# Gate and up pairs that move both parts of x side by side, and a pool product issued ahead of the scans

## The chip, the cores and the metric

The kernel runs on one core of one Trainium2 chip. The time is device time in microseconds (us) from one launch to its end; the median over runs is what is compared. In the profile TensorE is PE (its weight loads are PEld), VectorE is DVE, ScalarE is ACT, GpSimd is POOL, and SyncE is SP, which issues most of the transfers.

## The reference, cut to what matters

Two layers. Each is a feed-forward block, a mixer, and a second feed-forward block, each between two norms:

```python
for l in range(2):                                      # x: 256 tokens x 1024
    f = _swiglu(_rmsnorm(h, ff1_norm_pre[l]), wg, wu, wd)     # 1024 -> 2816 -> 1024
    h = h + 0.5 * _rmsnorm(f, ff1_norm_post[l])
    m = _hybrid_mixer(_rmsnorm(h, mix_norm_pre[l]), ...)
    h = h + _rmsnorm(m, mix_norm_post[l])
    f = _swiglu(_rmsnorm(h, ff2_norm_pre[l]), ...)
    h = h + 0.5 * _rmsnorm(f, ff2_norm_post[l])

def _swiglu(h, wg, wu, wd):
    return (silu(h @ wg) * (h @ wu)) @ wd

def _hybrid_mixer(h, w_in, ..., w_out):
    z, xbc, dt, u, q, k, v = split(h @ w_in)
    y_ssd  = _ssd_mixer(z, xbc, dt, ...)     # two chunks of 128 tokens, a state carried between them
    y_pool = _pool_mixer(u, pool_w, pool_scale)   # windowed means of u, minus u, times pool_w
    y_attn = _moba_attention(q, k, v)        # 256 tokens: one causal block
    return concatenate([y_ssd, y_pool, y_attn]) @ w_out
```

All inputs are float32. The kernel gets the precision from two-part products: every weight and every activation is held as a high part (`hi`, rounded to the format that TensorE takes) and a low part (`lo`, the rest), and a product is `hi.hi + hi.lo + lo.hi`.

## The kernel before

**Weights.** A weight unit is a tile `raw` of 128 x 2048 that SP loads. ACT copies it to `hi` (L104) and DVE subtracts to `lo` (L105). Four `raw` tiles and five pairs `hi`, `lo` exist at a time; `W.pump()` splits further units whenever a pair is free, so these splits run ahead of TensorE up to five units. Every split sits in the queues of ACT and DVE between the evacuations of the products.

**Feed-forward.** The 2816 hidden columns are eleven groups of 256. Groups 0 and 1 go token tile by token tile (`ffn_first`, L340). Groups in `QUADS = (2, 5, 8)` are taken two at a time as seven products of combined weights (`ffn_quad`, L469, with DVE sums at L103). Groups in `PAIRS = (4, 7, 10)` go through `ffn_pair`: gate unit `p["g", i]`, the transposes of the hidden values that were made before (`turn`, L446), up unit `p["u", i]`, and then the gate: SiLU of the gate bank on ACT (L417), its product with the up bank on DVE (L419), and a split of the result into `hT`. There are four feed-forwards and so twelve pairs. In a pair the products are made by `mm_feat` (L319): for each half of 128 columns (`j`) 24 matmuls of 256 columns, weight stationary, x turned (`xT`) moving, all into one accumulator of 256 columns: 8 for `hi` with the high part of x, 8 for `hi` with its low part, 8 for `lo` with the high part. So each `hi` tile is loaded twice. Down products (`mm_rows`, L358, into the banks called `acc`) follow.

**Mixer.** Late in the mixer stands a group of work that is ordered with `issue_after`: `scan(0)` and `scan(1)` (L926) are TensorE products of the two token chunks, `carry()` (L917, evacuated by DVE at L896 and L919) brings the state of chunk 0 into chunk 1, `gated` (L934 to L938) multiplies by silu(z) and normalizes, giving `yn0` and `yn1`, and the pool product (L967) gives `y_pool` after two scalings on ACT (L869) and a split (L219, L220). The output product then adds up, for token tile 0 and then for tile 1, the attention rows (`wa`), the pool rows (`wp`) and two SSD units (`ws0`, `ws1`), each 12 matmuls of 512 columns at L358. `gated_turn` transposes `yn0` and `yn1` for the SSD units (L944). When tile 0 is complete, `post(0)` normalizes it and adds it to `h`, the next block's pre-norm makes `xn0` (L227 squares and sums, L229 adds eps, POOL takes the power at L232, L251 updates `h`, L260 scales), and `pre_turn` transposes `xn0` (L270). That transpose is pinned in the middle of tile 1's last unit:

```python
mm_rows(acc[1], p["ws1"], 1, y_ssd[1], False, True, joint)    # joint: pre_turn(0, xn0)
```

**What sets the order.** The code is written in program order, with hints (`issue_after`); a list scheduler at build time then sets the order of each engine's queue, within the dependencies, and each engine runs its queue strictly in that order. Banks called `wk` and `acc` are two sets of four accumulators of 512 columns, and a new one waits until the last reader of the old one is done.

Of the kernel before, what the change touches and what calls it, by code (L numbers as in the profile page):

```python
# [11 lines left out]
F32R = mybir.dt.float32r  # L12
BF16 = mybir.dt.bfloat16
AF = mybir.ActivationFunctionType
ALU = mybir.AluOpType
AX = mybir.AxisListType

P = 128
D = 1024
S = 256  # L20
NT = S // P
DEPTH = 2
KD = D // P
# [6 lines left out]
UNIT = 2048  # L30
# [11 lines left out]
V_CW, V_CB, V_PS, V_PW = 0, 32, 40, 42  # L42
# [98 lines left out]
def hybrid_trunk_kernel(ctx: ExitStack, tc: tile.TileContext, a, out: bass.AP):  # L141
    nc = tc.nc
    consts = ctx.enter_context(tc.tile_pool(name="consts", bufs=1))
# [8 lines left out]
    def buf(dtype=F32, n=512, tag="t"):  # L152
        return tmp.tile([P, n], dtype, tag=tag, name=f"{tag}{next(ids)}", bufs={"t": 20, "n": 8}[tag])
# [4 lines left out]
    def bank(tag="wk"):  # L158
        return psum.tile([P, 512], F32, tag=tag, name=f"{tag}{next(ids)}")
# [4 lines left out]
    W = Weights(nc, rawp, splitp)  # L164
# [42 lines left out]
        nc.scalar.activation(neg_b, cst[:, C_NEG : C_NEG + P], AF.Copy)  # L207

    gains = consts.tile([P, 2, D], F32, name="gains")
    xT = [consts.tile([P, KD, S], F32R, name=f"xT{i}") for i in range(2)]  # L210

    def load_gain(which, l, n):
        row = a["gains"][l, n : n + 1, :]
# [99 lines left out]
    def mm_feat(ps, u, c, x=xT, ncols=256):  # L313

        hi, lo = (w[:, : KD * ncols].rearrange("p (k n) -> p k n", k=KD) for w in W.get(u))
        s = slice(c, c + P)
        for i, (w, y) in enumerate(((hi, x[0]), (hi, x[1]), (lo, x[0]))):
            for k in range(KD):
                nc.tensor.matmul(ps, w[:, k, s], y[:, k, :], start=i == 0 and k == 0, stop=i == 2 and k == KD - 1)  # L319

    def mm_tok(ps, u, t, ncols=256):

# [91 lines left out]
    def gate(pg, pu, s=None):  # L414
        if s is None:
            s = buf()
            nc.scalar.activation(s, pg, AF.Silu)  # L417
        hf = buf()
        nc.vector.tensor_tensor(hf, pu, s, op=ALU.mult)  # L419
        return hf  # L420
# [26 lines left out]
            split_into(hT[i], (slice(None), slice(None)), ps)  # L447

    def ffn_pair(i, p, turn):
        pg, pu = bank(), bank()  # L450
        for ps, k in ((pg, "g"), (pu, "u")):
            for j in range(2):
                mm_feat(ps[:, j * 256 : (j + 1) * 256], p[k, i], j * P)
            W.done(p[k, i])
            if k == "g":
                turn()
        hf = gate(pg, pu)
        hT = (buf(F32R), buf(F32R))
        split_into(hT, (slice(None), slice(None)), hf)
        W.pump()  # L460
        return hT
# [152 lines left out]
    def mixer(l, p, turned, next_left, before_next):  # L614
# [93 lines left out]
        turn = []  # L708
        for w in range(2):
            ps = bank("acc")  # L710
# [210 lines left out]
        def scan(t):  # L921
            ps = bank()
            for hd in range(HEADS):
                s = slice(hd * 64, (hd + 1) * 64)
                n = hd % 4
                scan.last = nc.tensor.matmul(ps[:, s], decay[t, hd // 4][:, n * P : (n + 1) * P], xdt[t][:, s],  # L926
                                             start=True, stop=True)
            return ps
# [27 lines left out]
        with tc.issue_after(turn_x.last.ins):  # L956
            sz1 = zed(1)
        with tc.issue_after(zed.last.ins):
            y0 = scan(0)
            yn0 = gated(0, y0, sz0)  # L960
            carry()
            y1 = scan(1)

            pp = bank("acc")
            pw = vec[:, V_PW : V_PW + 256].rearrange("p (j n) -> p j n", j=2)
            for j in range(2):
                m = nc.tensor.matmul(pp[:, j * 256 : (j + 1) * 256], pw[:, j, :], d[:, j, :], start=True, stop=True)  # L967
            y_pool = rows_out(pp, vec[:, V_PS : V_PS + 2])
            yn1 = gated(1, y1, sz1)
        acc = [banks2(), banks2()]  # L970
        with tc.issue_after(m.ins):
            mm_rows(acc[0], p["wa"], 0, y_attn, True, False)
        m = mm_rows(acc[0], p["wp"], 0, y_pool, False, False)
        with tc.issue_after(m.ins):
# [189 lines left out]
```

## Time and profile before

| | |
|---|---|
| time, median of 3 runs | 931.28 us (930.87 to 931.46) |
| the profiled execution, its own time | 931.69 us |
| its span, first to last instruction | 930.0 us |
| mean granted TensorE clock | 0.997 |
| PE busy | 917.9 us, 5058 matmuls |
| DVE busy | 785.5 us, 1019 instructions |
| ACT busy | 584.2 us, 931 instructions |
| POOL busy | 30.1 us, 49 instructions |
| memory | 190.54 MB in packets, mean 205 GB/s |

The span is 1.69 us shorter than the same execution's time, and that execution lies 0.41 us above the median. A matmul's duration in the profile overlaps the next one, so what a matmul costs in a row of them is read from start to start.

### The profile page before, as it was taken

Reading aid. Unit: us, or ns where it says so; the run is one execution under the profiler, and the core shown is the slowest. Engines: PE = TensorE matmul, PEld = TensorE weight load, DVE = VectorE, ACT = ScalarE, POOL = GpSimd, SP = SyncE. Lnnn points to the kernel's source line nnn. Section 1 sums busy time; section 2 is a strip of 40 time slices with the busy share of each in tenths; the row PEclk is TensorE's granted clock in tenths of the full one; section 3 lists DMA queues with packets and bytes.
Section 4 is the critical chain, followed back from the end, with each engine's and each line's share of the span. In section 5 each row is a group of like instructions: output and inputs, shape, how many; then the busy total and the mean of one; then the engine's idle time right before and its main releaser. Section 6 shows DMA issues by size and latency. Waiting matters only on the chain.

```text
span 930.0 us, 13066 instructions
## 1 busy us (share of the span) xinstructions
PE 917.9 (99%) x5058; PEld 794.0 (85%) x5058; DVE 785.5 (84%) x1019; ACT 584.2 (63%) x931; POOL 30.1 (3%) x49
## 2 busy tenths in 40 slices
PE   7999999999999999999999999999999999999997
PEld 5889898989988888888888988898998888989895
DVE  6999999589868998988599989876989699989872
ACT  7665747478738665646566756556794567656641
POOL 0000000000001000000000000000000110000000
PEclk9999999999999999999999999999999999999999
DMA  8576958465434486848455968583834246868521
GB/s 325 153 274 201 386 157 314 179 215 194 181 109 173 103 304 190 318 135 305 148 181 156 342 171 289 165 315 110 297 104 172 72 145 185 319 203 270 188 101 45
DMA packets 28002, 190.54 MB, mean 205 GB/s; under 512 B 3106, under 2 KB 3362, under 8 KB 5924
## 3 DMA queue, kind: packets, MB, share of 16 engines
q1 hardware_dynamic: 26068, 176.87, 52.1%
q0 software_dynamic: 1728, 12.58, 7.5%
q8 instruction: 39, 0.64, 0.3%
q10 hardware_dynamic: 144, 0.26, 0.1%
q14 instruction: 23, 0.19, 0.1%
HBM read 188.65 MB, written 1.05 MB: 204 GB/s over the span
## 4 chain that ended last, share of the span: by engine, by line
PE 95%; issue 1%; DVE 1%; DMA 1%; ACT 1%; POOL 0%; DVEq 0%; POOLq 0%; SPq 0%; ACTq 0%
PE acc L358 29%; PE wk L469 25%; PE wk L319 21%; PE wk L340 14%; PE wk L446 2%; PE wk L327 1%; PE wk L270 1%; DMA raw<-in_ff_f 1%; DVE lo L105 0%; PE acc L677 0%; PE acc L747 0%; ACT hi L104 0%; ACT n L227 0%; PE acc L879 0%; PE wk L905 0%
## 5 line engine op out<-in xcount | busy, mean ns | idle before, releaser
L104 ACT ACTIVATE hi<-raw 128x1024 fp32r<-128x1024 f32 (+2 forms) x452 | 401.1, 938 | 176.9 <-DVE raw L103 44.6
L105 DVE TENSOR_TENSOR lo<-raw,hi 128x1024 fp32r<-128x1024 f32 (+2 forms) x452 | 467.1, 1079 | 51.5 <-ACT hi L104 50.2
L358 PE MATMUL acc<-hi,t 128*128 128x512 f32 x832 | 216.2, 391 | 0.5 <-DVE t L896 0.5
L358 PEld LDWEIGHTS acc<-hi,t 128*128 128x128 f32 x832 | 154.8, 188 | 32.7 <-DVE t L896 1.4
L319 PE MATMUL wk<-xT,hi 128*128 128x256 f32 x1088 | 143.4, 284 | 0.0
L319 PEld LDWEIGHTS wk<-xT,hi 128*128 128x128 f32 x1088 | 136.7, 191 | 1.7
L358 PE MATMUL acc<-lo,t 128*128 128x512 f32 x416 | 114.1, 390 | 0.0
L469 PE MATMUL wk<-hi,n 128*128 128x512 f32 x384 | 102.9, 390 | 0.0
L340 PE MATMUL wk<-hi,xT 128*128 128x512 f32 x384 | 99.0, 395 | 2.6 <-ACT hi L104 2.6
L358 PEld LDWEIGHTS acc<-lo,t 128*128 128x128 f32 x416 | 78.0, 188 | 16.2
L103 DVE TENSOR_TENSOR raw<-raw,raw 128x1024 f32<-128x1024 f32 x72 | 86.2, 1219 | 1.9 <-DMA raw<-in_ff_q 1.9
L340 PEld LDWEIGHTS wk<-hi,xT 128*128 128x128 f32 x384 | 71.6, 189 | 17.6 <-ACT hi L104 3.4
L469 PEld LDWEIGHTS wk<-hi,n 128*128 128x128 f32 x384 | 71.8, 188 | 14.7
L469 PE MATMUL wk<-hi,xT 128*128 128x512 f32 x288 | 77.8, 392 | 0.0
L319 PE MATMUL wk<-xT,lo 128*128 128x256 f32 x544 | 76.8, 283 | 0.0
L319 PEld LDWEIGHTS wk<-xT,lo 128*128 128x128 f32 x544 | 70.3, 192 | 0.0
L469 PEld LDWEIGHTS wk<-hi,xT 128*128 128x128 f32 x288 | 53.5, 188 | 12.6 <-DVE t L502 1.8
L340 PE MATMUL wk<-lo,xT 128*128 128x512 f32 x192 | 52.3, 395 | 0.0
L469 PE MATMUL wk<-lo,n 128*128 128x512 f32 x192 | 51.3, 389 | 0.0
L244 DVE TENSOR_TENSOR n<-acc,gains 128x512 f32<-128x512 f32 x24 | 16.1, 689 | 33.6 <-ACT n L227 33.6
L340 PEld LDWEIGHTS wk<-lo,xT 128*128 128x128 f32 x192 | 36.6, 191 | 7.8
L469 PEld LDWEIGHTS wk<-lo,n 128*128 128x128 f32 x192 | 36.0, 188 | 7.5
(175 smaller groups left out, 731.2 us busy)
## 6 DMA issues: line engine op xcount, KB each, us to landing
raw<-in_ff_q SPq DMA_DIRECT2D x48, 1024.0 KB, 5.0
raw<-in_ff_d SPq DMA_DIRECT2D x44, 1024.0 KB, 5.0
raw<-in_ff_f SPq DMA_DIRECT2D x16, 1024.0 KB, 6.2
raw<-in_ff_q POOLq DMA_DIRECT2D x12, 1024.0 KB, 8.0
raw<-in_ff_g SPq DMA_DIRECT2D x12, 1024.0 KB, 4.8
raw<-in_ff_u SPq DMA_DIRECT2D x12, 1024.0 KB, 4.9
raw<-in_w_in SPq DMA_DIRECT2D x10, 1024.0 KB, 4.8
raw<-in_w_kvz SPq DMA_DIRECT2D x8, 1024.0 KB, 5.0
```

What stands on the lines that cost most here:

```text
L103: nc.vector.tensor_tensor(raw[:, s], self.raw[x][:, s], self.raw[y][:, s], op=op)
L104: self.act = nc.scalar.activation(hi[:, s], raw[:, s], AF.Copy)
L105: nc.vector.tensor_tensor(lo[:, s], raw[:, s], hi[:, s].bitcast(F32), op=ALU.subtract)
L244: nc.vector.tensor_tensor(fg[i], f[i], gains[:, 1, i * 512 : (i + 1) * 512], op=ALU.mult)
L270: pre_turn.last = nc.tensor.transpose(ps[:, k * P : (k + 1) * P], xn[i][:, k * P : (k + 1) * P], ident)
L319: nc.tensor.matmul(ps, w[:, k, s], y[:, k, :], start=i == 0 and k == 0, stop=i == 2 and k == KD - 1)
L327: nc.tensor.matmul(ps, x[:, k, s], w[:, k, :], start=i == 0 and k == 0, stop=i == 2 and k == KD - 1)
L340: m = nc.tensor.matmul(ps, y[:, k, :], w[:, k, :], start=h == 0 and n == 0, stop=h == 1 and n == len(parts) - 1)
L358: m = nc.tensor.matmul(acc[b], x[:, j, s], w[:, j, b * 512 : (b + 1) * 512], start=first and j == 0 and i == 0, stop=last and j == 1 and i ...
L446: nc.tensor.transpose(ps[:, j * S + t * P : j * S + (t + 1) * P], hf[t][:, c], ident)
L469: nc.tensor.matmul(ps, x[:, k, :], w[:, k, :], start=first and n == 0, stop=n == len(parts) - 1, skip_group_check=not first)
```

## The change

In `ffn_pair`, `mm_feat` is replaced by a new `mm_side`. The two parts of xT now lie in one tile, and `hi` moves both at once: 8 matmuls of 512 columns into one bank, the left half `hi.hi`, the right half `hi.lo`; 8 matmuls of 256 columns add `lo.hi` into the right half. ACT copies the right half out (L334) and DVE adds the left half to it (L335). This is done per 128 columns, so a unit takes two banks instead of one. SiLU and the product with the up values are now done on the summed copies.

```diff
-    xT = [consts.tile([P, KD, S], F32R, name=f"xT{i}") for i in range(2)]
+    both = consts.tile([P, 2, KD, S], F32R, name="xT")
+    xT = [both[:, i] for i in range(2)]
...
+    def mm_side(u, out):
+        hi, lo = (w[:, :UNIT].rearrange("p (k n) -> p k n", k=KD) for w in W.get(u))
+        for j in range(2):
+            s = slice(j * P, (j + 1) * P)
+            ps = bank()
+            for k in range(KD):
+                nc.tensor.matmul(ps, hi[:, k, s], both[:, :, k, :], start=k == 0, stop=k == KD - 1)
+            for k in range(KD):
+                nc.tensor.matmul(ps[:, S:], lo[:, k, s], xT[0][:, k, :], start=False, stop=k == KD - 1,
+                                 skip_group_check=True)
+            o = out[:, j * S : (j + 1) * S]
+            nc.scalar.activation(o, ps[:, S:], AF.Copy)
+            nc.vector.tensor_tensor(o, ps[:, :S], o, op=ALU.add)
+        W.done(u)
+        return out
...
     def ffn_pair(i, p, turn):
-        pg, pu = bank(), bank()
-        for ps, k in ((pg, "g"), (pu, "u")):
-            for j in range(2):
-                mm_feat(ps[:, j * 256 : (j + 1) * 256], p[k, i], j * P)
-            W.done(p[k, i])
-            if k == "g":
-                turn()
-        hf = gate(pg, pu)
+        s = mm_side(p["g", i], buf())
+        nc.scalar.activation(s, s, AF.Silu)
+        turn()
+        hf = mm_side(p["u", i], buf())
+        nc.vector.tensor_tensor(hf, hf, s, op=ALU.mult)
...
         with tc.issue_after(zed.last.ins):
+            pp = bank("acc")
+            pw = vec[:, V_PW : V_PW + 256].rearrange("p (j n) -> p j n", j=2)
+            for j in range(2):
+                pooled = nc.tensor.matmul(pp[:, j * 256 : (j + 1) * 256], pw[:, j, :], d[:, j, :], start=True, stop=True)
+            y_pool = rows_out(pp, vec[:, V_PS : V_PS + 2])
+        with tc.issue_after(pooled.ins):
             y0 = scan(0)
             yn0 = gated(0, y0, sz0)
             carry()
             y1 = scan(1)
-            pp = bank("acc")
-            ...
-            y_pool = rows_out(pp, vec[:, V_PS : V_PS + 2])
             yn1 = gated(1, y1, sz1)
         acc = [banks2(), banks2()]
-        with tc.issue_after(m.ins):
+        with tc.issue_after(scan.last.ins):
             mm_rows(acc[0], p["wa"], 0, y_attn, True, False)
```

The queues that come out of it differ as follows; line numbers are each version's own (L319 and L340 keep the meaning given above before; after the change L329 and L331 are the two loops of `mm_side`, L358 is `mm_half`, L376 is `mm_rows`, L271 the transposes of `xn`, L464 those of `hf`). Numbers behind a name count buffers.

PE, the first pair (group 4) of the second feed-forward, before: gate unit, the eight transposes of the hidden values, start of the up unit.

```order
L469 MATMUL wk_3098<-hi_3199,n_3119 128x512 x4
L319 MATMUL wk_3329<-xT_108,hi_3222 128x256 x8
L319 MATMUL wk_3329<-xT_109,hi_3222 128x256 x8
L319 MATMUL wk_3329<-xT_108,lo_3223 128x256 x8
L319 MATMUL wk_3329<-xT_108,hi_3222 128x256 x8
L319 MATMUL wk_3329<-xT_109,hi_3222 128x256 x8
L319 MATMUL wk_3329<-xT_108,lo_3223 128x256 x8
L446 MATMUL wk_3379<-ident,t_3242 128x128
```

The same place now.

```order
L484 MATMUL wk_3031<-hi_3132,n_3052 128x512 x4
L329 MATMUL wk_3263<-xT,hi_3155 128x512 x8
L331 MATMUL wk_3263<-xT,lo_3156 128x256 x8
L329 MATMUL wk_3282<-xT,hi_3155 128x512 x8
L331 MATMUL wk_3282<-xT,lo_3156 128x256 x8
L464 MATMUL wk_3302<-ident,t_3175 128x128
```

A unit's 48 matmuls of 256 columns have become 16 of 512 and 16 of 256, in two banks; nothing else moved there.

PE, the scan group of the first mixer, before (`t_2510` is the pooled difference d, `vec` holds pool_w).

```order
L926 MATMUL wk_2596<-t_2534,n_2272 128x64 x4
L926 MATMUL wk_2596<-t_2534,n_2277 128x64 x4
L917 MATMUL acc_2616<-t_2536,t_2306 128x256
L917 MATMUL acc_2616<-t_2536,t_2312 128x256
L926 MATMUL wk_2622<-t_2545,n_2282 128x64 x4
L926 MATMUL wk_2622<-t_2545,n_2287 128x64 x4
L967 MATMUL acc_2631<-t_2510,vec_860 128x256 x2
L358 MATMUL acc_2652<-hi_2295,t_2525 128x512
```

The same place now.

```order
L358 MATMUL wk_2482<-hi_2136,xT 128x512 x4
L977 MATMUL acc_2529<-t_2443,vec_837 128x256 x2
L941 MATMUL wk_2539<-t_2467,n_2205 128x64 x4
L941 MATMUL wk_2539<-t_2467,n_2210 128x64 x4
L932 MATMUL acc_2559<-t_2469,t_2239 128x256
L932 MATMUL acc_2559<-t_2469,t_2245 128x256
L941 MATMUL wk_2565<-t_2478,n_2215 128x64 x4
L941 MATMUL wk_2565<-t_2478,n_2220 128x64 x4
L376 MATMUL acc_2585<-hi_2228,t_2458 128x512
```

The pool product stands ahead of the scans.

PE, the same mixer from the last matmul of token tile 0 on, before: `wk_2713` takes the transposes of `yn1`, `acc_2654` and `acc_2655` are tile 1, `hi_2295` and `lo_2296` are `wa`, `hi_2400` is `wp`.

```order
L358 MATMUL acc_2653<-hi_2576,t_2470 128x512 x2
L944 MATMUL wk_2713<-ident,t_2650 128x128 x4
L358 MATMUL acc_2655<-lo_2296,t_2525 128x512
L358 MATMUL acc_2654<-hi_2295,t_2526 128x512
L358 MATMUL acc_2655<-hi_2295,t_2526 128x512
L358 MATMUL acc_2654<-hi_2295,t_2526 128x512
L358 MATMUL acc_2655<-hi_2295,t_2526 128x512
L358 MATMUL acc_2654<-hi_2400,t_2634 128x512
```

The same place now, where `hi_2333` is `wp` and `hi_2392` is `ws0`.

```order
L376 MATMUL acc_2586<-hi_2509,t_2403 128x512 x2
L959 MATMUL wk_2646<-ident,t_2583 128x128 x4
L376 MATMUL acc_2588<-hi_2333,t_2533 128x512
L376 MATMUL acc_2587<-hi_2333,t_2533 128x512
L376 MATMUL acc_2588<-hi_2333,t_2533 128x512
L376 MATMUL acc_2587<-hi_2392,t_2400 128x512
L376 MATMUL acc_2588<-hi_2392,t_2400 128x512
```

Before, tile 1 had had 7 of its matmuls when tile 0 was complete, and 35 more followed up to the transposes of `xn0`. Now it has had 21, and 21 follow up to the same transposes: 14 matmuls of `wa` and `wp` moved from behind the end of tile 0 to ahead of it. Both mixers have this order.

More of the change, by code (lines that the diff above doesn't have):

```diff
@@ L962, in mixer @@
             y1 = scan(1)
-            pp = bank("acc")
-            pw = vec[:, V_PW : V_PW + 256].rearrange("p (j n) -> p j n", j=2)
-            for j in range(2):
-                m = nc.tensor.matmul(pp[:, j * 256 : (j + 1) * 256], pw[:, j, :], d[:, j, :], start=True, stop=True)
-            y_pool = rows_out(pp, vec[:, V_PS : V_PS + 2])
             yn1 = gated(1, y1, sz1)
         acc = [banks2(), banks2()]
-        with tc.issue_after(m.ins):
+        with tc.issue_after(scan.last.ins):
             mm_rows(acc[0], p["wa"], 0, y_attn, True, False)
```

## The prediction

> **What bounds the kernel now.** I read the page's busy times first, then the waits of PE, then the timeline of PE through one pair and one mixer, and last the granted clock.
>
> ```profile
> PE 917.9 (99%) x5058; PEld 794.0 (85%) x5058; DVE 785.5 (84%) x1019; ACT 584.2 (63%) x931; POOL 30.1 (3%) x49
> PE wk L340 <- ACT hi L104: 2.6, 1, 2.6
> PE wk L199 <- DVE n L193: 2.3, 1, 2.3
> PE acc L358 <- DVE t L896: 0.5, 2, 0.3
> PE wk L270 <- DVE n L260: 0.5, 1, 0.5
> ```
>
> PE is busy for 99% of the span, and the list of its waits (total us, times, longest) has five: three at the start and one in each mixer. So everything that shortens PE's queue shortens the kernel, and every new wait of PE lengthens it, one for one. DVE is not far behind, so its extra work has to be looked at.
>
> **The pairs: the matmuls.** The timeline of PE through the first pair of the second feed-forward (start, length, count):
>
> ```profile
> 344.02 2.08 PE L319 MATMUL wk<-xT,hi 128*128 128x256 f32 x16
> 345.94 1.12 PE L319 MATMUL wk<-xT,lo 128*128 128x256 f32 x8
> 346.90 2.08 PE L319 MATMUL wk<-xT,hi 128*128 128x256 f32 x16
> 348.82 1.12 PE L319 MATMUL wk<-xT,lo 128*128 128x256 f32 x8
> 349.78 1.04 PE L446 MATMUL wk<-ident,t 128*128 128x128 f32 x8
> 276.15 1.52 PE L358 MATMUL acc<-hi,t 128*128 128x512 f32 x6
> 277.51 0.61 PE L358 MATMUL acc<-lo,t 128*128 128x512 f32 x2
> ```
>
> A unit's 48 matmuls of 256 columns take 349.78 - 344.02 = 5.76 us, 120 ns from start to start. Six of 512 columns take 277.51 - 276.15 = 1.36 us, 226.7 ns each. So one move of 512 columns costs 13.3 ns less than two of 256. Per unit 32 short ones become 16 long ones: 16 x 13.3 = 213 ns; 24 units: **-5.1 us**. The moving operand now has two pieces; no row shows that for this format, so I bound it. At best it runs as a single piece (-5.1). The nearest row is the masks' matmul, also moved in two pieces of 128:
>
> ```profile
> 222.88 0.61 PE L742 MATMUL acc<-b,b 128*128 128x256 bf16 x4
> 223.42 1.58 PE L747 MATMUL acc<-t,t 64*128 64x128 f32 x16
> ```
>
> (223.42 - 222.88) / 4 = 135 ns for 256 columns, 15 ns above L319; if all of that came from the second piece, 384 moves would lose 5.8 us and the gain would be gone (+0.7). But a change of operands stands in these four steps too, and pieces of 256 are longer, so I take -5.1.
>
> **The pairs: ACT and DVE.** A 256-column copy out of a bank and a 256-column pass of DVE over a bank have rows, and so have the weight splits that share these queues:
>
> ```profile
> L220 DVE TENSOR_TENSOR t<-wk,t 128x256 fp32r<-128x256 f32 x8 | 3.4, 419 | 0.9 <-ACT t L219 0.9
> L219 ACT ACTIVATE t<-wk 128x256 fp32r<-128x256 f32 x8 | 3.0, 379 | 2.9 <-DVE t L220 1.5 <-PE wk L944 1.5
> L419 DVE TENSOR_TENSOR t<-wk,t 128x512 f32<-128x512 f32 x20 | 13.7, 687 | 12.0 <-PE wk L319 12.0
> L104 ACT ACTIVATE hi<-raw 128x1024 fp32r<-128x1024 f32 x332 | 333.5, 1053 | 165.6 <-DVE raw L103 44.6 <-PE acc L358 24.7 <-PE wk L319 24.7
> ```
>
> Added: 48 x 0.419 = 20.1 us of DVE and 48 x 0.379 = 18.2 us of ACT, 1.7 and 1.5 us a pair; SiLU and the product stay. What hides them: ACT waits 24.7 us for L319 and as much for L358 before it splits, that is, all five split buffers are full and the next unit waits for PE. A pair is where the splits run ahead, so 1.7 us less lead costs PE nothing; if that cover were gone, it would be up to 12 x 1.7 = 20 us. The result's latency grows by a copy and an add (0.8 us) plus whatever split stands between; the hidden values of group 10 are first needed after two half down products (24 x 0.227 = 5.4 us behind the last up matmul), and the chain copy, add, split, product, copy, split comes to 0.4 + 0.4 + 0.7 + 0.7 + 0.6 + 2 x 0.7 + 0.7 = 4.9 us at most for the part needed last. The banks: the up unit's first bank is the gate's first, which DVE frees about a unit's half (2.8 us) earlier. One place has no cover: in the first feed-forward the splits run late, ACT's copies come between, and four down matmuls now stand ahead of the up unit and wait for their split. I take **+0.3**, between 0 and one evacuation of 0.6.
>
> **The mixer: what goes away.** The same timeline:
>
> ```profile
> 268.05 1.07 PE L358 MATMUL acc<-hi,t 128*128 128x512 f32 x4
> 269.37 2.11 PE L358 MATMUL acc<-hi,t 128*128 128x512 f32 x8 [0.25 <-DVE t L896]
> 279.79 0.60 PE L944 MATMUL wk<-ident,t 128*128 128x128 f32 x4
> 287.72 0.62 PE L358 MATMUL acc<-hi,t 128*128 128x512 f32 x2
> 288.18 1.03 PE L270 MATMUL wk<-ident,n 128*128 128x128 f32 x8
> 724.63 2.11 PE L358 MATMUL acc<-hi,t 128*128 128x512 f32 x8 [0.26 <-DVE t L896]
> ```
>
> Four matmuls from 268.05 end their turn at 268.05 + 4 x 0.227 = 268.96, and the next starts at 269.37: PE waits 0.4 us for the bank that `carry` held until L896. Now `wp` stands in that place, ready since the pool product is first, and tile 1 begins 12 matmuls later: **-0.4 a mixer, -0.8**. The moved product's own work on ACT and DVE (L869, L219, L220) now runs ahead of `gated` on DVE; that makes `yn0` about 1.7 us later, but its transposes come 12 matmuls' worth (2.7 us) later or so too. No transfer moves with the product, and SP's queue keeps its order; `wa` is done earlier, so its split buffer is free earlier and a split of the next block comes forward on ACT.
>
> **The mixer: what is late next.** Tile 0 is complete at 279.79. The chain to `xn0`:
>
> ```profile
> 279.99 0.60 ACT L227 ACTIVATE n<-acc 128x512 bf16<-128x512 f32 x1 [0.29 <-PE acc L358]
> 281.86 1.41 DVE L251 SCALAR_TENSOR_TENSOR h<-n,s,h 128x512 f32<-128x512 f32 x2
> 285.36 0.28 ACT L229 ACTIVATE s<-s,s 128x1 f32<-128x1 f32 x1
> 285.71 0.87 POOL L232 TENSOR_TENSOR s<-s,halfexp 128x1 f32<-128x1 f32 x1 [3.89 <-ACT s L229]
> 286.62 1.42 DVE L260 SCALAR_TENSOR_TENSOR n<-h,s,gains 128x512 f32<-128x512 f32 x2 [0.44 <-POOL s L232]
> ```
>
> The first half of `xn0` is there at 286.62 + 0.71 = 287.33, 7.5 us after tile 0, the second at 288.04, 8.25 us after. PE came to L270 at 288.18, 8.4 us after: its 35 matmuls just covered the chain. Of these, 14 now lie ahead of tile 0's end, so PE comes after 8.4 - 14 x 0.227 = 5.2 us and waits 7.5 - 5.2 = 2.3 us, and 0.2 more between the two halves, since four transposes (0.44) are shorter than the 0.67 between them. ACT's queue in that stretch has one split more ahead of the second norm, 0.2 to 0.4 us. Bounds 2.3 and 2.9; I take 2.7: **+5.4** for two mixers. Queued behind L270 are the last six matmuls of tile 1 and the next block's first products, and for them ACT and DVE wait with the splits of xT; all go on at their old distances, only later, so nothing of the wait is won back.
>
> **The mixer: the clock.** A wait of that length was there once, at the start. Windows of the trace (length, PE busy, granted clock, DMA) and PE's timeline behind it:
>
> ```profile
> 6.38:9.80 3.42, 2.43 (x11) 1.00 0.98 410
> 9.80:13.21 3.41, 1.29 (x4) 1.00 1.02 430
> 13.21:16.62 3.41, 3.41 (x9) 0.50 0.80 315
> 16.62:20.00 3.38, 3.38 (x16) 1.00 0.91 327
> 15.02 1.83 PE L340 MATMUL wk<-lo,xT 128*128 128x512 f32 x4
> 16.69 2.00 PE L340 MATMUL wk<-hi,xT 128*128 128x512 f32 x8
> 18.52 1.07 PE L340 MATMUL wk<-lo,xT 128*128 128x512 f32 x4
> ```
>
> After a stretch of 3.41 us with PE idle for 2.1 the clock was granted by half for the next 3.41 us; after one with 1.0 us idle it was not. At half clock a matmul took (16.69 - 15.02) / 4 = 0.42 us, then (18.52 - 16.69) / 8 = 0.23, so such a stretch loses 3.41 x (1 - 0.23 / 0.42) = 1.5 us. If stretches follow each other every 3.41 us, a wait of 2.6 puts 2.1 or more into one of them for (3.41 - 2.6 + 2 x 0.5) / 3.41 = 53% of positions; with a limit nearer to 1.0, always. The two mixers lie 724.63 - 269.37 = 455.3 us apart, 133.4 stretches, so their positions differ by 0.4: likeliest, one of the two waits is followed by half clock: **+1.5**.
>
> The Trainium skill, page "TensorE: Matmul & The Clock Gate", section "What's actually happening", says that the clock falls only after at least one idle window of about 3.4 us. By that rule a wait of 2.7 us costs itself alone. The length agrees with the rows, but the window of 9.80 to 13.21 was not idle and the clock still fell, so I give this rule the smaller chance.
>
> **The sum.** -5.1 + 0.3 - 0.8 + 5.4 + 1.5 = +1.3 us on the span of 930.0: 931.3. With the 1.69 us around it the execution takes 933.0, and set against the median, 0.41 below the profiled execution, **932.6 us**, 0.14% above. 0.2%, 1.9 us, is about what a measurement of this kernel can tell from no change.
>
> **Rivals.** *Both waits are followed by half clock*: 934.1 us, slower by 0.30%. For it: a limit below 2.1 us; against it: the positions. It decides from +0.6 us more than my sum. *No half clock*: 931.1, no change. The Trainium skill's rule above gives this time. *The moves in two pieces are not cheaper*: the change then does not do what it says, 932.6 + 5.1 = 937.7, and 935 at half the gain; for it speaks L742 alone. *The turn's wait does not appear*, because the norm's chain gets shorter with fewer splits between: at most -5.1 + 0.3 - 0.8, 925.7. Against it: of the 7.5 us, only about 1 is other work on ACT. It turns to faster once the wait is below 1.8 us a mixer without half clock.
>
> **How the numbers follow.** One half clock 43%, none 22%, both 16%, dearer moves or new waits in the pairs 9%, shorter wait at the turn 10%. No change takes the 22%, most of the 43% and little of the others, 0.59; slower is 'both', the dear moves and the upper edge of the likeliest, 0.30; faster is the last case, 0.11. The range 930.2 to 934.5 holds the first three cases with their terms' bounds (2 x 0.4 at the turn, 0.3 in the pairs) and leaves the last two out.
>
> **What would show it.** The two loops of `mm_side` at 227 and 120 ns from start to start, 5.55 us a unit; the wait for L896 gone; a wait of PE for the scaling of `xn0` of 2.3 to 2.7 us in each mixer, the longest after the start; a granted clock of 0.50 in a stretch of 3.41 us behind one of them. DVE near 806 us. Wrong, if that wait is under 1.8 us, if PE waits for L335, or if the two-piece moves take more than 235 ns.

## The result and the profile after

The changed kernel takes **936.97 us** (median of 4 runs, 935.54 to 937.8) against 931.08 us (930.83 to 931.46) for the kernel before beside it: ratio **1.0061**, 95% interval 1.0044 to 1.0079. It is slower by 5.9 us; forecast was 932.6, with 930.2 to 934.5 as range. The profiled execution took 937.24 us, its span is 935.5, 5.5 above before.

The page's busy times and the list of PE's waits after the change (total us, times, longest):

```profile
PE 917.5 (98%) x4674; PEld 776.6 (83%) x4674; DVE 802.2 (86%) x1067; ACT 602.2 (64%) x979; POOL 31.7 (3%) x49
PE wk L271 <- DVE n L261: 5.4, 3, 2.5
PE wk L199 <- DVE n L193: 2.3, 1, 2.3
PE wk L358 <- ACT hi L104: 2.2, 1, 2.2
PE wk L484 <- DVE t L517: 1.1, 1, 1.1
PE wk L484 <- DVE wk L510: 0.7, 1, 0.7
PE acc L376 <- ACT t L220: 0.2, 1, 0.2
```

The waits for L896 are gone. Of the three at the transposes (L271) one, of 0.4 us, is at the start and was there before (0.5); the two of 2.5 us are new, stand at the transposes of `xn0` in the mixers, and were forecast. Also new are 1.8 us at L484, in a place that the prediction does not name: one quad of the first feed-forward. PE's busy time hardly fell although 384 matmuls are fewer: a matmul at half clock counts as busy for longer, and in the last version below, which has no half clock in the mixers and no wait in that quad, it is 913.0.

PE in the first pair of the second feed-forward after the change (start, length, count):

```profile
349.01 1.98 PE L329 MATMUL wk<-xT,hi 128*128 128x512 f32 x8
350.82 1.11 PE L331 MATMUL wk<-xT,lo 128*128 128x256 f32 x8
351.78 2.00 PE L329 MATMUL wk<-xT,hi 128*128 128x512 f32 x8
353.62 1.11 PE L331 MATMUL wk<-xT,lo 128*128 128x256 f32 x8
354.57 1.03 PE L464 MATMUL wk<-ident,t 128*128 128x128 f32 x8
```

From 349.01 to 350.82 stand eight long moves, (350.82 - 349.01) / 8 = 226 ns each: the operand in two pieces costs nothing that the rows show (226.7 ns before). A unit takes 354.57 - 349.01 = 5.56 us where it took 5.76.

PE's timeline at the two waits in the mixers:

```profile
288.53 0.61 PE L376 MATMUL acc<-hi,t 128*128 128x512 f32 x2
291.65 1.97 PE L271 MATMUL wk<-ident,n 128*128 128x128 f32 x8 [2.50 <-DVE n L261]
745.30 0.61 PE L376 MATMUL acc<-hi,t 128*128 128x512 f32 x2
748.42 1.84 PE L271 MATMUL wk<-ident,n 128*128 128x128 f32 x8 [2.50 <-DVE n L261]
```

Two matmuls from 288.53 end their turn at 288.98, and the transposes start at 291.65: 2.67 us, the same in the second mixer. Windows of the same places (from:to, length, PE busy and matmuls, granted clock, DMA share, GB/s), cut on the grid of 3.41 us on which the granted clock changes:

```profile
287.95:291.37 3.42, 1.20 (x6) 1.00 0.20 43
291.37:294.78 3.41, 3.13 (x12) 0.50 0.68 271
294.78:298.19 3.41, 3.41 (x17) 1.00 0.02 8
745.34:748.75 3.41, 0.91 (x6) 1.00 0.31 65
748.75:752.17 3.42, 3.42 (x12) 0.50 0.59 244
```

In both mixers a stretch with 2.2 to 2.5 us of PE idle is followed by one at half clock. The two halved stretches start 748.75 - 291.37 = 457.38 us apart, 134 times 3.413.

The quad of the first feed-forward that lost time, groups 8 and 9: PE at its first product, at the waits and behind it, before and after.

```profile
138.76 1.07 PE L469 MATMUL wk<-hi,xT 128*128 128x512 f32 x4
157.82 1.07 PE L358 MATMUL acc<-hi,t 128*128 128x512 f32 x4
```

```profile
137.93 1.07 PE L484 MATMUL wk<-hi,xT 128*128 128x512 f32 x4
152.41 1.17 PE L484 MATMUL wk<-hi,n 128*128 128x512 f32 x4 [0.72 <-DVE wk L510]
155.77 1.20 PE L484 MATMUL wk<-hi,xT 128*128 128x512 f32 x4 [1.06 <-DVE t L517]
159.31 1.07 PE L376 MATMUL acc<-hi,t 128*128 128x512 f32 x4
```

The quad took 19.06 us and takes 21.38, 2.3 more. So the span's 5.5 is: 24 units at -0.20 = -4.8; the first feed-forward +0.6 at its first pair (0.5 of it, from start to start, the wait for `hT`'s split) and +2.3 in that quad; in the mixers +5.3 for the two waits, +0.5 at the second halves of their transposes, -0.8 for `carry`'s bank, some +2.8 for two stretches of half clock; -0.4 in the start, which the change does not touch. Sum +5.5. What of this is cause was tested.

### The profile page after: what moved, and what is told of

Its sections match the earlier page's. It is cut to its first block, busy times and chain, and to the rows that moved or that the text cites. A ratio compares the mean times of both kernels' runs of the same rounds, so it can differ in the third digit from the quotient of the medians.

```text
span 935.5 us, 12407 instructions
## 1 busy us (share of the span) xinstructions
PE 917.5 (98%) x4674; PEld 776.6 (83%) x4674; DVE 802.2 (86%) x1067; ACT 602.2 (64%) x979; POOL 31.7 (3%) x49
## 4 chain that ended last, share of the span: by engine, by line
PE 92%; ACT 2%; DMA 2%; issue 2%; DVE 2%; POOL 0%; DVEq 0%; POOLq 0%; SPq 0%; ACTq 0%
PE acc L376 27%; PE wk L484 23%; PE wk L358 14%; PE wk L329 9%; PE wk L320 6%; PE wk L331 5%; PE wk L464 1%; PE wk L271 1%; PE wk L345 1%; ACT hi L104 1%; DMA raw<-in_ff_q 1%; DMA raw<-in_ff_f 1%; PE wk L941 1%; DVE lo L105 1%; ACT n L228 0%
## 5 line engine op out<-in xcount | busy, mean ns | idle before, releaser
L376 PE MATMUL acc<-hi,t 128*128 128x512 f32 x832 | 217.8, 393 | 0.2 <-ACT t L220 0.2
L376 PEld LDWEIGHTS acc<-hi,t 128*128 128x128 f32 x832 | 155.3, 189 | 32.2 <-ACT t L220 1.2
L376 PE MATMUL acc<-lo,t 128*128 128x512 f32 x416 | 114.2, 391 | 0.0
L484 PE MATMUL wk<-hi,n 128*128 128x512 f32 x384 | 102.3, 390 | 0.7 <-DVE wk L510 0.7
L358 PE MATMUL wk<-hi,xT 128*128 128x512 f32 x384 | 99.2, 396 | 2.2 <-ACT hi L104 2.2
L329 PE MATMUL wk<-xT,hi 128*128 128x512 f32 x384 | 96.8, 394 | 0.0
L376 PEld LDWEIGHTS acc<-lo,t 128*128 128x128 f32 x416 | 78.6, 189 | 16.7
L358 PEld LDWEIGHTS wk<-hi,xT 128*128 128x128 f32 x384 | 72.1, 191 | 16.9 <-ACT hi L104 2.4
L484 PEld LDWEIGHTS wk<-hi,n 128*128 128x128 f32 x384 | 71.7, 188 | 15.7 <-ACT hi L104 1.1
L329 PEld LDWEIGHTS wk<-xT,hi 128*128 128x128 f32 x384 | 69.8, 188 | 13.0
L484 PE MATMUL wk<-hi,xT 128*128 128x512 f32 x288 | 77.4, 391 | 1.1 <-DVE t L517 1.1
L484 PEld LDWEIGHTS wk<-hi,xT 128*128 128x128 f32 x288 | 53.8, 188 | 13.2 <-DVE t L517 2.2
L331 PEld LDWEIGHTS wk<-xT,lo 128*128 128x128 f32 x384 | 52.4, 190 | 3.7
L331 PE MATMUL wk<-xT,lo 128*128 128x256 f32 x384 | 53.5, 282 | 0.0
L484 PE MATMUL wk<-lo,n 128*128 128x512 f32 x192 | 51.8, 389 | 0.0
L358 PE MATMUL wk<-lo,xT 128*128 128x512 f32 x192 | 51.6, 391 | 0.0
L320 PE MATMUL wk<-xT,hi 128*128 128x256 f32 x320 | 42.5, 283 | 0.0
L358 PEld LDWEIGHTS wk<-lo,xT 128*128 128x128 f32 x192 | 36.0, 188 | 7.8 <-DVE lo L105 0.2
```

Of the source, the lines that this page charges most:

```text
L329: nc.tensor.matmul(ps, hi[:, k, s], both[:, :, k, :], start=k == 0, stop=k == KD - 1)
L331: nc.tensor.matmul(ps[:, S:], lo[:, k, s], xT[0][:, k, :], start=False, stop=k == KD - 1, skip_group_check=True)
L358: m = nc.tensor.matmul(ps, y[:, k, :], w[:, k, :], start=h == 0 and n == 0, stop=h == 1 and n == len(parts) - 1)
L376: m = nc.tensor.matmul(acc[b], x[:, j, s], w[:, j, b * 512 : (b + 1) * 512], start=first and j == 0 and i == 0, stop=last and j == 1 and i ...
L484: nc.tensor.matmul(ps, x[:, k, :], w[:, k, :], start=first and n == 0, stop=n == len(parts) - 1, skip_group_check=not first)
```

## Experiments

Each theory's numbers stand in the text that was written before the run; "before" beside the runs was 930.8 to 931.1 us.

**The two halves of the change apart.** The pairs alone on the mixer of before; then the moved pool product alone with the old pairs.

> The kernel before with only the pairs in the new form; the mixer's order is that of before. Before 931.1, after 937.0 us. Theory A (the account read from the two traces): the 384 long moves save 5.1 us and the first feed-forward gives 2.8 back (0.4 where its first pair's down product waits for a split, 2.2 in its last quad, whose splits come late, 0.2 beside them): 931.1 - 5.1 + 2.8 = 928.8, with PE waiting for DVE in the first feed-forward's last quad at about 151 and 154 us, and in none of the other feed-forwards. Rival B (the waits of that quad are an accident of the profiled execution, or come from the start): 931.1 - 5.1 + 0.4 = 926.4. Rival C (moves in two pieces are not cheaper): 931 or more.

> The kernel before with only the pool product moved ahead of the scan; the pairs are the old ones. Theory A: the bank's wait goes (-0.4 a mixer), the turn of tile 0 is waited for (2.7 a mixer), and half clock follows each of the two waits (1.5 each): 931.1 + 2 x (2.7 - 0.4 + 1.5) = 938.7. Rival B (half clock comes behind one wait only, as predicted): 937.2. Rival C (no half clock; the third part of after's loss lies elsewhere): 935.7. Rival D (the loss belongs to the pairs, the moved product costs nothing): 930.3.

The pairs alone: 928.95 us, ratio 0.9977 (0.9967 to 0.9987), theory A, and PE's waits in that quad are there again without any change in a mixer. The pool product alone: 937.32 us, ratio 1.0070 (1.0055 to 1.0086), with the same two waits. In PE's timeline of the profiled execution:

```profile
289.41 1.38 PE L270 MATMUL wk<-ident,n 128*128 128x128 f32 x8 [2.50 <-DVE n L260]
748.93 1.38 PE L270 MATMUL wk<-ident,n 128*128 128x128 f32 x8 [2.50 <-DVE n L260]
```

And windows on its grid of the clock; half clock followed the first wait and not the second:

```profile
287.46:290.87 3.41, 1.36 (x10) 1.00 0.63 211
290.87:294.28 3.41, 3.41 (x10) 0.50 0.25 101
744.84:748.26 3.42, 1.59 (x8) 1.00 0.17 22
748.26:751.67 3.41, 2.65 (x15) 1.00 0.72 288
```

The same wait of 2.5 us lay with 2.05 us in one stretch the first time; the second time it was cut by a stretch's end into 1.83 and 0.76, and the clock stayed. So in this execution B occurs, one half clock, and in the changed kernel's A's two do, by the position. The slowest of the four runs, 939.59 us with a mean clock of 0.993 where the others have 0.995 or 0.996, fits A; its trace was not kept. The half that only moves an order costs more than all that the other half saves.

**Is it PE's idling that halves the clock?** Dead matmuls in the wait, 11 and then 5 of them:

```diff
         def joint():
-            pre_turn(0, xn0, left=next_left)
+            spare, w1 = bank(), W.get(p["ws1"])[0]
+            for _ in range(11):        # 5 in the second version
+                dead = nc.tensor.matmul(spare, y_ssd[1][0][:, :P], w1[:, :512], start=True, stop=True)
+                tc.keep_in_program_order(dead)
+            with tc.issue_after(dead.ins):
+                pre_turn(0, xn0, left=next_left)
             return pre_turn.last
```

> After, with 11 matmuls of 512 columns, whose result nobody reads, put on PE just ahead of the transposes of xn0 in each mixer (11 x 0.227 = 2.5 us, the length of the wait). Nothing is computed earlier, so the turn itself comes no sooner. Theory A (PE's idling in that wait brings the half clock): no stretch of 0.50 in the mixers, 1.4 to 1.5 us less in each: 937.0 - 2.9 = 934.1. Rival B (the half clock has another cause, such as the load before it): still 0.50 behind both, 937.0. Rival C (the wait is not that of the norm's chain but follows PE's own position): the fillers add to it, 937.0 + 5.0 = 942.

> After, with 5 matmuls of 512 columns, whose result nobody reads, in the wait ahead of the transposes of xn0 in each mixer instead of 11: PE is idle there for about 2.66 - 5 x 0.227 = 1.5 us in one piece instead of 2.66 or 0.2. Theory A (the clock is granted by half when PE idles for more than some 1.8 to 2.0 us of a stretch of 3.41 us): 1.5 is below it in every position, no half clock in the mixers, 934.0 as with 11 fillers, since the wait ends when xn0 is ready in both. Rival B (the length of the idle piece or another limit decides): half clock still in one or both, 935.5 to 937.

With 11: 933.99 us (7 runs, 932.85 to 934.6), 3.0 below the changed kernel. With 5: 934.64 us (4 runs, 934.13 to 935.03). Windows of the two, in the mixers' waits:

```profile
286.70:290.12 3.42, 3.32 (x16) 1.00 0.27 46
290.12:293.53 3.41, 3.38 (x19) 1.00 0.64 264
```

```profile
288.55:291.97 3.42, 1.96 (x10) 1.00 0.29 46
291.97:295.38 3.41, 3.37 (x19) 1.00 0.63 264
```

No half clock in either, as theory A said, and `xn0` was no sooner there. The medians put the two halved stretches at 3.0 and 2.3 us; they hold other differences too, since in the profiled execution with 11 PE waits only 0.7 us in the quad. The traces are the better measure: from the first transpose to the next block's first matmul the changed kernel takes 3.8 us in the first mixer and 4.0 in the second, the version with five dead matmuls 2.5 in both. Half clock thus costs 1.3 and 1.5 us, 2.8 together; the start's rows had said 1.5 each. Five useless matmuls are enough: the 1.46 us idle in a stretch of the first mixer, and 1.49 in the second, are below the limit.

**Is the order of tile 1 the whole cost in the mixer?** The pool product stays first, and tile 1's matmuls from the sixth (then: from the tenth) on are queued behind tile 0's last.

```diff
-    def mm_rows(acc, u, t, xs, first, last, between=None):
+    def mm_rows(acc, u, t, xs, first, last, between=None, behind=None):
...
-            m = nc.tensor.matmul(acc[b], ...)
+            with tc.issue_after(behind.ins) if behind and n >= 5 else nullcontext():    # 9 in the second
+                m = nc.tensor.matmul(acc[b], ...)
...
-        mm_rows(acc[0], p["ws1"], 0, y_ssd[1], False, True)
+        done0 = mm_rows(acc[0], p["ws1"], 0, y_ssd[1], False, True)
-        mm_rows(acc[1], p["wa"], 1, y_attn, True, False)
+        mm_rows(acc[1], p["wa"], 1, y_attn, True, False, behind=done0)
```

> After, with the out projection's tile 1 held back: only the first five of its matmuls may run before tile 0's last matmul, the others are queued behind it; the pool product stays first. 37 matmuls then lie between tile 0's end and the turn of xn0 (37 x 0.227 = 8.4 us, and 0.35 of transposes) instead of 21. Theory A (the order of these matmuls is the whole cost in the mixer): no wait at the turn, no half clock, 937.0 - 2 x (2.7 + 1.4) = 928.8. Rival B (a new wait at the first matmuls of ws0, which come 0.9 us behind the turn of yn0 and need its split): up to 1 us a mixer, 930.8. Rival C (the chain is late for another reason than the order of tile 1): still a wait over 2 us, 937.

> As the version with tile 1 held back behind its fifth matmul, but behind its ninth: 8 of them stand between the turn of yn0 and ws0 instead of 4, and 33 instead of 37 between tile 0's end and the turn of xn0. In the version before, PE waited 0.8 us in each mixer for the split of yn0 and came to the turn of xn0 1.55 us after it was ready. Theory A (both waits can be had covered at once): 0.8 us less in each mixer, 929.3 - 1.6 = 927.7, and no wait over 0.2 us in the mixers. Rival B (the split of yn0 slips by as much, since ACT takes another weight split ahead of it): 929.3. Rival C (the turn of xn0 is then late again): up to 930 and a wait of PE for it.

Held behind the fifth: 929.3 us, ratio 0.9978 (0.9969 to 0.9988), 7.7 below the changed kernel: the wait at L271 and the half clock are gone, with the pool product still first. A part of rival B came: PE waits 0.8 us a mixer for the split of `yn0`.

```profile
274.52 1.20 PE L377 MATMUL acc<-hi,t 128*128 128x512 f32 x4 [0.63 <-ACT t L220]
288.97 1.04 PE L271 MATMUL wk<-ident,n 128*128 128x128 f32 x8
289.76 0.71 PE L377 MATMUL acc<-hi,t 128*128 128x512 f32 x2
```

Behind the ninth that wait is gone too, and the wait in the quad of the first feed-forward is all that its list holds after the start besides 0.2 us; yet the time is 928.82 us (9 runs, 927.45 to 929.76), 0.5 less where 1.6 was expected. The runs of both versions spread over 2 us, more than the difference, but the timeline shows where the rest went:

```profile
287.96 0.61 PE L377 MATMUL acc<-hi,t 128*128 128x512 f32 x2
288.55 1.38 PE L271 MATMUL wk<-ident,n 128*128 128x128 f32 x8
289.69 0.70 PE L377 MATMUL acc<-hi,t 128*128 128x512 f32 x2
```

Two matmuls from 287.96 end their turn at 288.41, so the transposes start 0.14 us late, and they take 1.14 us to the next matmul where the version held behind the fifth takes 289.76 - 288.97 = 0.79. That is 0.5 us at the turn of `xn0`, the same in the second mixer, in two pieces that PE's list leaves out. So rival C came in small: of the 1.6 us won at `yn0`, 1.0 was lost again at `xn0`, since four matmuls fewer cover its chain.

**What is late in the quad?** The weights of a quad's seven products are `g1`, `g2`, `u2` and four combined ones, T1 to T4. First, on the mixer of before, the evacuations without the long moves, that is, PE's work of before with the new load on ACT and DVE; then the pairs with group 7 of the first feed-forward in the old form.

```diff
-            for k in range(KD):
-                nc.tensor.matmul(ps, hi[:, k, s], both[:, :, k, :], start=k == 0, stop=k == KD - 1)
+            for y in range(2):
+                for k in range(KD):
+                    nc.tensor.matmul(ps[:, y * S : (y + 1) * S], hi[:, k, s], xT[y][:, k, :], start=k == 0, stop=k == KD - 1)
```

```diff
+        if first and i == 7:                  # first: l == 0 and n == 1
+            pg, pu = bank(), bank()
...
+            hf = gate(pg, pu)
+        else:
             s = mm_side(p["g", i], buf())
```

> Only the pairs' new evacuation: the kernel before, with each unit's result put together by ACT's copy and DVE's add out of two bank halves, but with the old 256-column moves (each half of x moved by itself into its half of the bank), so PE's work is that of before. The mixer is that of before. Before 930.9, the pairs alone with long moves 928.95 us. Theory A (the extra 20 us of DVE and 18 us of ACT are hidden except in the first feed-forward, where the splits run late): PE's own time is unchanged, the first pair's wait of 0.4 stays, and in the last quad PE arrives 0.85 later than with long moves, so of the 2.2 us there 1.3 stay: 930.9 + 0.4 + 1.3 = 932.6. Rival B (the quad's lateness comes only of PE arriving earlier through shorter moves): 930.9 + 0.4 = 931.3. Rival C (the evacuations cost something in every pair, hidden in e_pairs' sum): 930.9 + 24 x 0.2 = 935 or more.

> The pairs alone on the mixer of before (928.95 us), but in the first feed-forward the middle pair, group 7, keeps the old form, so its ACT and DVE work is that of before; the 11 other pairs are new. Theory A (that pair's two evacuations more on ACT and DVE delay the sum for T1, the accumulating transfer behind it and T3's split, for which PE then waits in the last quad): the quad's 2.1 us go and the pair's own gain of 0.43 is lost: 927.3. Rival B (it is the loss of lead over the whole feed-forward, from both pairs): about half of the wait stays, 928.3. Rival C (the quad's wait has nothing to do with pairs): 929.4.

The evacuations alone: 931.46 us, ratio 1.0007 (0.9998 to 1.0017). Theory A fell: the 20 us of DVE and 18 of ACT alone are hidden to within 0.7 us, and PE does not wait in that quad, only 0.5 us at the first pair and 0.2 in a quad of the third feed-forward. So the load alone does not do it. The time is rival B's (931.3), but the run does not show B, PE's earlier arrival, either: the order of ACT's queue at this place is that of the kernel before. With the old group 7: 927.25 us, theory A's 927.3, and no wait in that quad (its trace has one of 0.9 us in the third feed-forward instead). That run does not tell load from order, since the old pair also gives back the old order of ACT's queue. That order, at this place, in the kernel before and in the changed one (`hi31` is T2's split, `hi32` T3's):

```
before:
L104 ACTIVATE hi31_1189<-raw23_968 128x1024
L219 ACTIVATE t96_1176<-t95_1174 128x512
L104 ACTIVATE hi31_1189<-raw23_968 128x1024
L104 ACTIVATE hi32_1221<-raw24_991 128x1024 x2
after:
L104 ACTIVATE hi31_1144<-raw23_945 128x1024
L220 ACTIVATE t100_1131<-t97_1091 128x512
L104 ACTIVATE hi32_1176<-raw24_968 128x1024
L104 ACTIVATE hi31_1144<-raw23_945 128x1024
L104 ACTIVATE hi32_1176<-raw24_968 128x1024
```

`raw24` is the tile into which POOL's transfer (L109) adds the weights for T3. Its issue, and ACT and DVE behind it, before and after:

```profile
125.46 0.87 POOL L109 DMA_DIRECT2D raw<-in_ff_q  x1 [43.09 <-DVE raw L103]
133.57 2.02 ACT L104 ACTIVATE hi<-raw 128x1024 fp32r<-128x1024 f32 x2 [2.33 <-PE acc L358]
```

```profile
126.93 0.87 POOL L109 DMA_DIRECT2D raw<-in_ff_q  x1 [44.46 <-DVE raw L103]
136.25 4.86 ACT L104 ACTIVATE hi<-raw 128x1024 fp32r<-128x1024 f32 x5 [4.36 <-DMA raw<-in_ff_q]
137.34 3.50 DVE L105 TENSOR_TENSOR lo<-raw,hi 128x1024 fp32r<-128x1024 f32 x3 [3.59 <-ACT hi L104]
```

The transfer is issued 1.5 us later, behind the later sum, and takes 9.2 us from issue to landing where it took 7.9; why it takes longer, no run shows. Before, it landed at 133.4, just ahead of T3's split at 133.57, which PE's freeing of a buffer released. Now it lands at 136.1. ACT stands 4.4 us in front of it with T2's second half, whose input is ready, queued behind, and DVE stands 3.6 us behind ACT. From 137 us to the quad's end DVE then has no gap left, and its sums for the quad (L510, L517) come late. Two versions change that order alone. The first holds T3's split behind T2's; the second exchanges two jobs, so that the split of `g2`, which waits for no such transfer, stands ahead of T3's:

```diff
                 p["T3", i] = W.job(u1, free=(u1,))
+                if l == 0 and n == 1 and i == 8:
+                    W.behind.add(p["T3", i])      # its first split: issue_after(the last split on ACT)
```

```diff
-                p["T3", i] = W.job(u1, free=(u1,))
                 g2 = W.unit(src[2])
-                p["g2", i] = W.job(g2)
+                if l == 0 and n == 1 and late:
+                    p["g2", i] = W.job(g2)
+                    p["T3", i] = W.job(u1, free=(u1,))
+                else:
+                    p["T3", i] = W.job(u1, free=(u1,))
+                    p["g2", i] = W.job(g2)
```

> The pairs alone on the mixer of before (928.95 us), all twelve in the new form, with one thing changed: in the first feed-forward's last quad (group 8), T3's split is held behind both halves of T2's on ACT. In the pairs alone ACT's queue has T2's first half, T3's first half, T2's second half; T3's first half waits for the accumulating transfer, and T2's second half, ready 4 us earlier, stands behind it. DVE's queue follows ACT's in the same four instructions; nothing else moves on any engine. Theory A (this swap in the queue makes the splits late, and PE waits 2.1 us in that quad): the waits at 151 and 154 us go, 928.95 - 2.1 = 926.9. Rival B (the extra ACT and DVE work itself makes them late, the swap only goes with it): 928.9 or at most 0.5 less. Rival C (half: the transfer still lands too late for T3): 927.9, one wait left at T3's or u2's product.

> The pairs alone on the mixer of before (928.95 us), all twelve new; in the first feed-forward's last quad the split of g2 comes ahead of T3's in the order of jobs. On ACT g2's two halves then stand where T3's stood, and T3's, which wait for the accumulating transfer, come behind them; on DVE the sum for T4 comes ahead of T3's split, as in the kernel before. No instruction is added or left out, and PE's order is the same. Theory A (the rest of the quad's wait comes of ACT and DVE standing idle behind the late transfer with work behind it that was ready): DVE's idle time of 2.3 us at 137 us goes, and with it both waits of PE in that quad: 928.95 - 2.1 = 926.9. Rival B (ACT and DVE simply have too much to do there, 1.7 us more than before): the wait left by holding T3 behind T2 stays, 928.2.

Holding T3 back gives the old order again: 928.25 us, 0.7 of the 2.1, nearest to rival C. The first of the two waits goes, the other stays, and ACT still waits for the transfer, which takes 9.1 us here too:

```profile
154.19 1.20 PE L488 MATMUL wk<-hi,xT 128*128 128x512 f32 x4 [0.78 <-DVE t L521]
135.80 4.08 ACT L106 ACTIVATE hi<-raw 128x1024 fp32r<-128x1024 f32 x4 [3.05 <-DMA raw<-in_ff_q]
```

The exchange: **926.54 us**, ratio 0.9950 (0.9936 to 0.9963), theory A, with all the extra work of ACT and DVE in place. DVE's timeline in it:

```profile
133.23 4.62 DVE L105 TENSOR_TENSOR lo<-raw,hi 128x1024 fp32r<-128x1024 f32 x4
137.78 2.35 DVE L103 TENSOR_TENSOR raw<-raw,raw 128x1024 f32<-128x1024 f32 x2
140.05 7.09 DVE L105 TENSOR_TENSOR lo<-raw,hi 128x1024 fp32r<-128x1024 f32 x6
```

And the list of PE's waits after the start:

```profile
PE acc L376 <- DVE t L915: 0.5, 2, 0.3
PE acc L376 <- ACT t L220: 0.2, 1, 0.2
```

DVE runs through from 133 us on without a gap where it stood for 3.6 us, and PE waits nowhere in the quad. So the quad's loss comes of a transfer that lands 2.7 us later than before together with queues that stand behind it. T3 ahead of T2's second half is 0.7 us of it; the rest comes in the old order too, where T3's late split stands ahead of that of `g2`. The exchanged order is not that of the kernel before, and it takes the whole loss away with all the extra work in place.

**Versions put together.** All with the pool product first and tile 1 held behind its ninth matmul: old pairs in groups 4 and 7 of the first feed-forward; T3 held behind T2; the same with an old group 4; and the exchanged jobs.

> The pool product first, tile 1 held back behind its ninth matmul, and new pairs everywhere but in the first feed-forward's groups 4 and 7, which keep the old form. Theory A: 930.9 - 5.1 + 2 x 0.43 (two pairs without the gain) - 2 x 0.4 (the bank's wait in the mixers) = 925.9, no wait of PE over 0.3 us after the start. Rival B (the first feed-forward's waits stay for another cause): 928. Rival C (group 4 in the old form brings new waits later, or the mixer keeps 0.8 each): 927.5.

> The pool product first, tile 1 held back behind its ninth matmul (928.8 us), all twelve pairs new, and T3's split of the first feed-forward's group 8 held behind T2's on ACT. Theory A (the swap alone makes the quad late): 928.8 - 2.1 = 926.7. Rival B (the evacuations' work makes it late): 928.8. Against the version with two old pairs (927.0): it has 0.86 more of short moves saved and keeps 0.6 of waits around the first pair, so 926.7 by that way too.

> As the one before, but the first feed-forward's group 4 keeps the old form of the pair, where the new one makes PE wait 0.4 us for a split of the down product and loses 0.2 beside it. Theory A: 0.6 gained and 0.43 of saved moves lost: 926.5. Rival B (the first pair's loss is small change, or another place waits instead): 926.9 or more.

> The same exchange of two jobs in the version with the pool product first and tile 1 held back behind its ninth matmul (928.8 us), all twelve pairs new. Theory A: 928.8 - 2.1 = 926.7, with one wait of PE left after the start, 0.2 us at the first pair's down product. Rival B: 928.0, as with T3 held behind T2.

They took 927.0 us (0.9957, 0.9942 to 0.9972), 928.02 (0.9967, 0.9955 to 0.9980), 926.91 (0.9959, 0.9946 to 0.9971) and **926.48** (0.9951, 0.9938 to 0.9963). The first missed theory A by 1.1: PE's list has no wait left after the start, but the turn of `xn0` costs 0.5 us a mixer as in the version held behind the ninth (its trace has the same 0.14 and 1.14). The second is as far from A as the pairs with T3 held back. The third came to rival B's 926.9, with a wait of 0.7 us in the third feed-forward. The last keeps all twelve new pairs and the pool product first, and after the start its list has only the wait at the first pair. Its busy times and its last two waits (L271 is that of the start):

```profile
PE 913.0 (99%) x4674; PEld 774.2 (84%) x4674; DVE 801.5 (87%) x1067; ACT 602.0 (65%) x979; POOL 31.0 (3%) x49
PE wk L271 <- DVE n L261: 0.8, 1, 0.8
PE acc L377 <- ACT t L220: 0.2, 1, 0.2
```

Against the pairs with exchanged jobs on the mixer of before it gains 0.06 us, not measurable, though two waits of 0.4 for `carry`'s bank are gone: its transposes of `xn0` lose the same 0.5 us a mixer. In this form the moved pool product is worth nothing that these runs can show.

## Why the prediction was wrong, by its own steps

**The pairs' matmuls** (-5.1): right. The rows say 226 ns for a long move and 5.56 us a unit, 24 x 0.20 = -4.8; the rival of dearer moves is out. With the quad mended, the pairs are worth 931.13 - 926.54 = 4.6 us.

**The pairs' ACT and DVE work** (+0.3): this step failed, by 2.5 us. The 0.5 in the first pair is as described. What the step took for cover, "five split buffers are full", is a sum over four feed-forwards. In the changed kernel's trace it held in three, where PE does not wait. In the first, T3's split of the last quad had, in the kernel before, 0.2 us between its transfer's landing and its start; there the pair's work shifted the sum for T1, the transfer behind it, and the build-time order of ACT's queue, until a split that was ready stood behind one that waited. The prediction itself called that feed-forward the place without cover and then costed one evacuation there. The work as such was as harmless as predicted (0.7 us in the run with the evacuations alone, not clear of nothing); the queue behind the POOL transfer was not looked at.

**The mixer's bank wait** (-0.8): right; no wait for `carry`'s evacuation appears with the pool product first.

**The turn of `xn0`** (+5.4): right in place and nearly in size, 2 x 2.67 us, and 0.2 to 0.3 at each second half. Holding tile 1 back took it away. It is late mainly since tile 1 ran ahead of tile 0, as the step said; the chain itself grew from 7.5 us to 8.0 (from 283.58 to 291.55 in the first mixer), about as the step had allowed.

**The half clock** (+1.5): the mechanism was right, the size was not: two stretches, 2.8 us. The limit was not at fault: the stretches of the changed kernel had 2.22 and 2.50 us idle, above the start's 2.1 (in the mixers 2.05 idle halved the clock and 1.83 did not). The positions were: they were taken from before, 455.3 us apart. The wait itself and the half clock move the second one later, the six shorter pairs between move it back by 2.4, and 748.42 - 291.65 = 456.8 us are left, 133.8 stretches, nearly the same position, and both waits were followed by half clock. With the pool product alone (748.93 - 289.41 = 459.5, 134.6 stretches) one was. Where the first wait would fall on the grid could not be known beforehand, so part of this miss is luck. Both waits with half clock was a rival at 16%; with 1.3 more for it and 2.5 for the quad, the sum comes to 936.4.

The Trainium skill, page "TensorE: Matmul & The Clock Gate", section "What's actually happening", has the clock fall after an idle window of about 3.4 us, and the windows free-running. The length and the free run agree with these traces (3.41 us, on one grid over the whole span); that the window must be idle does not, since 0.91 to 1.36 us of PE's work stood in the mixers' windows that were followed by half clock.

## What to carry to other kernels

Work that is hidden on average has to be hidden where the lead is shortest: look up the place with the least time between a transfer's landing and its first use, and there follow the queue behind that transfer, since one instruction that waits for a late transfer holds up all that is ready behind it. A reordering that frees a small wait can spend the cover of a larger one: count the matmuls between the start of a chain and its end, before and after. Look for waits in the steps from start to start as well as in a list: two pieces of 0.14 and 0.35 us were in no list. A wait of 2.7 us on TensorE here cost 4 us where it left 2.0 us or more of a stretch idle, and five dead matmuls in it kept the clock at full.

## What was not expected of the hardware

The grant of the clock looks at fixed stretches of 3.41 us, not at the length of a wait. PE's idle time in a stretch of the mixers, and the clock in the next one: 2.50, 2.22 and 2.05 gave 0.50; 1.83, 1.49 and 1.46 gave 1.00. So the same wait costs 2.7 or about 4 us by where it falls, and it may fall otherwise in the next run: of the four runs of the changed kernel three had a mean clock of 0.993, and the fourth, the fastest with 935.54 us, 0.997; no trace of that one was kept. The limit is not one number: at the start 1.71 to 2.70 us idle gave 0.50 in these executions (1.71 with the exchanged jobs, 2.70 with five dead matmuls), and up to 1.64 gave 1.00 (with the old group 7). What makes the difference is open.
